# Stores of the transposed x1 in sixteen steps, down weights loaded behind the last form of x, and another order of operands in the out projection

## The chip, the cores and the metric

The kernel runs on one core of a Trainium2 chip. The metric is the device time of one execution in microseconds (us). The five engines of the core run their own instruction streams in order: TensorE (PE, matrix products), VectorE (DVE), ScalarE (ACT), GpSimd (POOL) and SyncE (SP, which here issues nearly all transfers). They meet through semaphores only.

## The reference

One layer of a decoder trunk on x of 1024 tokens by 1024 features, float32:

```python
x = x + gla_mixer(rms_norm(x, norm_mix), w_in, w_gk_up, b_gk, g_onorm, w_out)
x = x + sqrelu_mlp(rms_norm(x, norm_ffn), w_ff1, w_ff2)      # square(relu(h @ w_ff1)) @ w_ff2
return rms_norm(x, final_norm)
```

The mixer is a gated linear attention whose last product is `(o * silu(r)) @ w_out`. The MLP has 4096 hidden features.

## The kernel before, in words

**Products.** Every big product is 1024 x 1024 x 1024 in float32, computed as a Strassen-like scheme of seven steps (`step`, `chunks_of`): each step multiplies one *form* (a block, or a sum of blocks, of the left side) with one form of the right side. Each operand form is 512 x 512, kept as two buffers of the tag `big` (half 0 and half 1 of the contracted dimension), and each buffer holds a high part (written by ACT, L81) and the remainder (written by DVE, L82). A product of high and low parts takes three matmuls, so a step has 48 matmuls of 128 x 512: half 0 for four lanes, then half 1. There are eight `big` buffers, enough for the step that runs and the one that is made.

**Plan.** After the projections and the attention, `plan` lists nine products: the out projection (number 0), then for each of four chunks c of 1024 hidden features an *up* product (w_ff1, into the hidden tiles `hq`) and a *down* product (w_ff2, added to the result). They are called up0, down0, up1, down1 and so on here. During step `at` of product i, `operand` makes the forms of the next step: sums of blocks first, then the split into high and low. The letters of `turns` set the order in which the parts of an operand are written into the program: "W" splits the weights, "n" makes the weight sums for the step after, "x" and "X" sum and split the other side. Other engines than PE are ordered by a scheduler from that program; PE's order is written by hand.

**The other side of an up product.** up0 makes the seven forms of x1 and stores them to DRAM (`xw`). up1, up2 and up3 load them back (class `Stored`, L1030, two transfers of 1 MB for each step) and do no sums.

**Weights.** Weights of the next product are loaded in steps 5 and 6 (`load`, ahead of the operand in the program). Each is four blocks called 11, 12, 21, 22 of two halves with 512 KB; up weights use the tags wa (11, 21, and the temporary t) and wb (12, 22), down weights wb (11, 21) and wa (12, 22, and t). For down products the sums of weight blocks run on POOL: t = 12 - 11 for step 1, then t = 22 - t and 12 = 22 - 12 for step 2, later t = 21 - t, each in two halves. POOL also sums the up weights of up1 to up3.

**Transposing x1.** The residual x1 lies in DRAM by features (`xh`) and is needed by tokens (`xm`) at the end. For each of eight tiles of 128 features, `turn_load` loads it (L976), `turn_blocks` transposes 32 x 32 blocks on DVE (L980), and `turn_store` writes it to `xm` with four transfers of 32 x 32 x 32 elements, 128 KB each (L987). Before, each tile takes three neighbouring steps and a new tile starts at every step, from the last step of down0 to the second of down1. All these transfers, the loads of `xw` and the weights are issued by SP, in order.

Of the kernel before, what the change touches and what calls it, by code (L numbers as in the profile page):

```python
# [25 lines left out]
NC = FF // 1024  # L26
# [14 lines left out]
def order_after(tc, inst, other, wait=True):  # L41

    kind = mybir.DependencyClass.Sync if wait else mybir.DependencyClass.NoSync
    tc.add_manual_dep(inst.ins, other.ins.name, mybir.DependencyInfo(kind, mybir.DependencyReason.DATA),
                      reason="order of phases")
# [3 lines left out]
def hybrid_trunk(ctx: ExitStack, tc: tile.TileContext, x, xT, w_head, w_r, w_gk, w_up,  # L49
                 w_out, w_ff1, w_ff2, vecs, g_fin, out):  # L50
    nc = tc.nc
# [25 lines left out]
    last = {}  # L77
# [41 lines left out]
    def run(general):  # L119
# [8 lines left out]
        def half(hf):  # L128
            return slice(hf * 512, hf * 512 + 512)
# [102 lines left out]
        def step(n, lhs, rhs, sink, by_lane=False, between={}, fine=False):  # L232

            b = BANK[n]

            def product(lane, kp):
                kh, k = kp // 2, kp % 2
                if n in (0, 1, 5) and kp == 0:
                    bank[b, lane] = new("gl" if b == "U" or lane == 0 else "mm")
                ls = slice(lane * P, lane * P + P)  # L240
                mm3(bank[b, lane], lhs[kh][:, k, 0, ls], lhs[kh][:, k, 1, ls], rhs[kh][:, k, 0, :], rhs[kh][:, k, 1, :],
                    n in (0, 1, 5) and kp == 0, n in (3, 5, 6) and kp == 3, True)
                if kp == 3:
                    sink(n, lane, bank[b, lane])

            if by_lane:
                for lane in range(4):
                    for kp in range(4):
                        product(lane, kp)
                        for f in between.get((lane, kp), ()):  # L250
                            f()
            elif fine:
                for kp in range(4):
                    for lane in range(4):
                        product(lane, kp)
            else:
                for kh in range(2):
                    for lane in range(4):
                        product(lane, 2 * kh)
                        product(lane, 2 * kh + 1)  # L260

        def chunks_of(plan, ops, hooks, sinks, last_by_lane=False, turns={}):

            def operand(i, at):

                which, order = plan[i][2], plan[i][4]
                w, x_ = plan[i][which], plan[i][1 - which]
                made = {}  # L270
                for turn in turns.get((i, at), ("W", "n", "x", "X") if which == 0 else ("x", "X", "W", "n")):
                    if callable(turn):
                        turn()
                    elif turn == "x":
                        x_.sums(order[at])
                    elif turn == "X":
                        made[1 - which] = x_.split(order[at])
                    elif turn == "w":
                        w.sums(order[at])
                    elif turn == "W":  # L280
                        made[which] = w.split(order[at])
                    elif at + 1 < len(order):
                        w.sums(order[at + 1])
                return made[0], made[1]

            def load(i, names):
                if i < len(plan):
                    w = plan[i][plan[i][2]]
                    for name in names[w.s_form]:
                        w.load(name)  # L290

            if not ops:
                ops.append(operand(0, 0))
            for i, (_, _, _, sink, order) in enumerate(plan):
                for at, n in enumerate(order):
                    for f in hooks.get((i, at), ()):
                        f()
                    cur = ops.pop(0)
                    if at == 5:
                        load(i + 1, {True: ("11", "12"), False: ("11", "12", "22")})  # L300
                    if at == 6:
                        load(i + 1, {True: ("21", "22"), False: ("21",)})
                    nxt = (i, at + 1) if at + 1 < len(order) else (i + 1, 0)
                    if nxt[0] < len(plan):
                        ops.append(operand(*nxt))
                    for f in hooks.get((i, at, "then"), ()):
                        f()
                    here = {k[2:]: v for k, v in hooks.items() if len(k) == 4 and k[:2] == (i, at)}
                    final_step = last_by_lane and (i, at) == (len(plan) - 1, 6)
                    step(n, *cur, sinks.get((i, at), sink), bool(here) or final_step, here, (i, at) in fine_steps)  # L310
# [176 lines left out]
        class KeptX:  # L487

            s_form = False
# [297 lines left out]
        def g(f, *args):  # L787
            return lambda: f(*args)
# [44 lines left out]
        def r_last():  # L833

            for n in R_LAST:
                wr[n] = wR.split(n)
                if n == R_LAST[0] or not general:
# [4 lines left out]
        hooks = {(0, 1): (gk_first,), (0, 1, "then"): (gk_first_out,), (0, 3): (split_up,),  # L842
                 (0, 4): (g(token_rms, range(0, 4)),), (0, 5): (g(token_rms, range(4, 8)),),
                 (1, 0, 0, 3): (g(spread_rms, 0),),
                 (2, 4): (r_last,),
                 (1, 2): (x12_load,), (1, 4): (x12_split,), (1, 5): (g(gk_second, 0),),
                 (1, 5, 1, 3): (g(gk_second, 1),), (1, 5, 2, 3): (g(spread_rms, 1),)}
        if not general:
# [10 lines left out]
                          (2, 0, 3, 3): (g(prep_fast, 2, 1),), (2, 3, "then"): (g(prep_fast, 3, 1),),  # L859
                          (2, 4, 2, 1): (g(operands, 0, "mm"),)})  # L860
        chunks_of([(wqk, xq, 0, qk_into, PLAIN), (xk, wv, 1, v_into, PLAIN), (xr_, wR, 1, r_into, R_FIRST)], ops_a, hooks, {},
                  turns={(0, 1): ("X", split_gate, "W"), (0, 2): ("x", "X", "w", "W", lambda: last.update(sums=last["split"], s1=last["sum"], s1_low=last["low"]), "n"),
                         (0, 3): ("W", "x", "X", "n"), (2, 3): ("x", "X", "W", g(wR.sums, 3))})
# [58 lines left out]
        def from_down(c):  # L922
            def bring(a, b, kh, dst):
                f0 = 8 * c + 4 * a + 2 * kh
                nc.sync.dma_start(dst.rearrange("p (k n) -> p k n", k=2),
                                  w_ff2[f0:f0 + 2, :, half(b)].rearrange("k p n -> p k n"))
            return bring


# [33 lines left out]
        ops = [[wo.split(0), so.split(0)]]  # L963
# [8 lines left out]
        turn = {}  # L972
# [7 lines left out]
            dve.transpose(u, turn[kt])  # L980
            turn[kt] = u

        def turn_store(kt):
            u = turn.pop(kt)
            for q_ in range(4):
                dst = xm[:, kt * P + 32 * q_:kt * P + 32 * q_ + 32].rearrange("(b i) j -> i b j", i=32)
                store = nc.sync.dma_start(dst, u[32 * q_:32 * q_ + 32, :].rearrange("p (b j) -> p b j", j=32))  # L987
                order_after(tc, store, last["xw"], wait=False)
# [25 lines left out]
        xw = [[dram.tile([P, 2048], F32, name=f"xw{n}{kh}{int(general)}") for kh in range(2)] for n in range(7)]  # L1014
# [3 lines left out]
                nc.sync.dma_start(xw[n][kh], tiles[kh].rearrange("p k l t -> p (k l t)").bitcast(F32))  # L1018

        class Stored:  # L1020
            s_form = False

            def sums(self, n):
                pass
# [75 lines left out]
        plan = [(wo, so, 0, onto_x1T, PLAIN)]  # L1100
# [5 lines left out]
        def load_gfin():  # L1106
# [3 lines left out]
        hooks = {(0, 0, 3, 3): [g(outputs_T, TT - 1, ("mm", "mm"))],  # L1110
                 (0, 4, "then"): [g(times_g, "11", lane) for lane in range(4)], (2 * NC - 2, 0): [load_gfin]}

        for k in range(KT):
            for i, at, f in ((2 * NC - 6, 6 + k, turn_load), (2 * NC - 6, 7 + k, turn_blocks), (2 * NC - 6, 8 + k, turn_store),
                             (2 * NC - 2, 5 + k, x1_load), (2 * NC - 2, 7 + k, x1_onto)):
                hooks.setdefault((i + at // 7, at % 7, "then"), []).append(g(f, k))
        chunks_of(plan, ops, hooks, {}, last_by_lane=True)

    flag = sb.tile([P, 1], I32, name="flag")
    with tc.manual_schedule(engines={mybir.EngineType.PE}):  # L1120
        run(False)
# [66 lines left out]
```

## Time and profile before

| | before |
|---|---|
| runs | 1010.89 us median of 3 (1007.34 to 1010.99) |
| profiled execution, own time | 1010.57 us |
| its span, first to last instruction | 1008.7 us |
| granted TensorE clock, mean | 0.993 of full speed |
| HBM read and written | 146.62 MB and 46.14 MB |

The page's second part shows the span in 40 slices, a digit for each (the busy share in tenths); the three rows below are those of VectorE, GpSimd and the sixteen DMA engines. A slice is 25.2 us long, so the slices 23 to 25 are 555 to 630 us.

```profile
DVE  6995796778889999699564369974349966569965
POOL 0000010113430000214043033224141224242270
DMA  9899785576382257660336996344961125970004
```

The rows say which engines are loaded in which stage; what ends a wait is read from the groups and the timeline.

### The profile page before, as it was taken

To read this page: it belongs to the slowest core of one execution; us is meant where nothing else is said; L and a number is where in the kernel's file an instruction comes from. 1 tells how busy PE (TensorE), PEld (TensorE's weight loads), DVE (VectorE), ACT (ScalarE), POOL (GpSimd) and SP (SyncE) were. 2 spreads that over 40 slices of the span, in tenths; PEclk is the share of its full clock that TensorE was granted. 3 is DMA by queue.
4 is the path that set the end of the run, shared out by engine and by line. 5 is a ranking of instruction groups with operands and counts; after the bars stand their busy time and mean duration, and the time that the engine had idled before them with its cause. 6 is when DMAs were issued, how large, how long until landed. Compare 5 with 4: busy or idle time off the path is not lost.

```text
span 1008.7 us, 12239 instructions
## 1 busy us (share of the span) xinstructions
PE 986.9 (98%) x4508; PEld 821.5 (81%) x4508; DVE 752.5 (75%) x899; ACT 564.9 (56%) x858; POOL 229.3 (23%) x142
## 2 busy tenths in 40 slices
PE   9999999999999999999999989999999999999995
PEld 7788878889988888888888868888888888888884
DVE  6995796778889999699564369974349966569965
ACT  7685554787784466666434454332447333556455
POOL 0000010113430000214043033224141224242270
PEclk9999999999999999999999999999999999999998
DMA  9899785576382257660336996344961125970004
GB/s 264 314 322 369 288 294 193 204 247 209 118 286 78 84 209 292 250 233 19 89 136 232 273 323 136 90 120 174 340 250 49 53 73 210 363 285 39 1 1 171
DMA packets 135694, 193.65 MB, mean 192 GB/s; under 512 B 39240, under 2 KB 100808, under 8 KB 124104
## 3 DMA queue, kind: packets, MB, share of 16 engines
q1 hardware_dynamic: 135064, 192.37, 55.3%
q8 instruction: 37, 0.61, 0.2%
q10 hardware_dynamic: 560, 0.40, 0.1%
q14 instruction: 33, 0.27, 0.1%
HBM read 146.62 MB, written 46.14 MB: 191 GB/s over the span
## 4 chain that ended last, share of the span: by engine, by line
PE 78%; DVE 2%; DMA 2%; ACT 1%; issue 1%; SPq 0%; DVEq 0%; ACTq 0%
PE gl L70 53%; PE mm L70 24%; DMA big<-xw 1%; DMA wb<-in_w_out 1%; DVE big L82 1%; DVE vx L1074 0%; PE mm L636 0%; DMA wb<-in_w_ff 0%; ACT g L696 0%; PE mm L715 0%; ACT wb L81 0%; DVE vx L950 0%; PE gl L715 0%; DVE g L1094 0%; DVE g L705 0%
## 5 line engine op out<-in xcount | busy, mean ns | idle before, releaser
L70 PE MATMUL gl<-big,big 128*128 128x512 f32 x2712 | 632.5, 391 | 6.5 <-DMA big<-xw 4.5
L70 PEld LDWEIGHTS gl<-big,big 128*128 128x128 f32 x2712 | 510.2, 188 | 114.2 <-ACT big L81 5.7
L70 PE MATMUL mm<-big,big 128*128 128x512 f32 x1224 | 288.6, 389 | 0.2 <-ACT g L810 0.2
L70 PEld LDWEIGHTS mm<-big,big 128*128 128x128 f32 x1224 | 229.7, 188 | 48.3 <-ACT g L810 0.6
L82 DVE TENSOR_TENSOR big<-wa,big 128x1024 fp32r<-128x1024 f32 (+1 forms) x118 | 156.7, 1353 | 85.1 <-ACT big L81 81.3
L81 ACT ACTIVATE big<-wa 128x1024 fp32r<-128x1024 f32 (+1 forms) x118 | 118.3, 1039 | 116.1 <-PE gl L70 59.3
L184 POOL TENSOR_TENSOR wa<-wa,wa 128x1024 f32<-128x1024 f32 x28 | 78.8, 2821 | 145.7 <-DVE big L82 144.9
L184 POOL TENSOR_TENSOR wa<-wa,wb 128x1024 f32<-128x1024 f32 x14 | 42.9, 3069 | 296.9 <-DVE big L82 258.9
L82 DVE TENSOR_TENSOR big<-wb,big 128x1024 fp32r<-128x1024 f32 x50 | 63.3, 1284 | 34.8 <-ACT big L81 34.8
L82 DVE TENSOR_TENSOR big<-hq,big 128x1024 fp32r<-128x1024 f32 x48 | 61.4, 1291 | 34.9 <-ACT big L81 34.8
L81 ACT ACTIVATE big<-wb 128x1024 fp32r<-128x1024 f32 x50 | 51.0, 1052 | 58.2 <-PE gl L70 26.6
L81 ACT ACTIVATE big<-hq 128x1024 fp32r<-128x1024 f32 x48 | 48.6, 1052 | 45.4 <-PE gl L70 21.9
L81 ACT ACTIVATE big<-raw 128x1024 fp32r<-128x1024 f32 x42 | 43.3, 1056 | 52.2 <-DVE raw L184 22.1
L82 DVE TENSOR_TENSOR big<-raw,big 128x1024 fp32r<-128x1024 f32 x42 | 67.2, 1620 | 4.5 <-ACT big L81 4.3
L556 POOL COPY top<-g 128x4 f32<-128x4 f32 x8 | 10.1, 1264 | 181.7 <-DVE g L548 181.7
L184 POOL TENSOR_TENSOR wa<-wb,wa 128x1024 f32<-128x1024 f32 x14 | 41.1, 2945 | 40.0 <-DVE big L82 40.0
L1009 ACT ACTIVATE hq<-hq 128x1024 f32<-128x1024 f32 x24 | 25.4, 1057 | 36.5 <-DVE hq L1002 36.5
L678 POOL TENSOR_SCALAR g<-g,est 128x256 f32<-128x256 f32 x28 | 29.1, 1056 | 52.0 <-DVE g L675 33.0
L1000 ACT ACTIVATE hq<-gl 128x512 f32<-128x512 f32 x36 | 21.3, 593 | 20.2 <-PE gl L70 20.1
L70 PE MATMUL gl<-wb,wa 128*128 128x256 f32 x180 | 32.1, 310 | 0.0
L1047 DVE TENSOR_TENSOR vx<-gl,vx 128x512 f32<-128x512 f32 x44 | 29.1, 681 | 0.9 <-PE gl L70 0.8
L70 PEld LDWEIGHTS gl<-wb,wa 128*128 128x128 f32 x180 | 26.3, 190 | 2.0
(201 smaller groups left out, 884.5 us busy)
## 6 DMA issues: line engine op xcount, KB each, us to landing
big<-xw SPq DMA_DIRECT2D x42, 1024.0 KB, 7.1
big<-xv SPq DMA_DIRECT2D x20, 1024.0 KB, 5.8
xv<-big SPq DMA_DIRECT2D x14, 1024.0 KB, 8.6
xw<-big SPq DMA_DIRECT2D x14, 1024.0 KB, 4.8
wa<-in_w_ff SPq DMA_DIRECT2D x32, 256.0 KB, 4.1
wb<-in_w_ff SPq DMA_DIRECT2D x32, 256.0 KB, 3.4
wa<-in_w_ff SPq DMA_DIRECT2D x16, 512.0 KB, 5.2
wb<-in_w_ff SPq DMA_DIRECT2D x16, 512.0 KB, 5.1
```

Of the source, the lines that this page charges most:

```text
L70: pe.matmul(o, w, m, start=start, stop=stop, skip_group_check=partial)
L81: last["split"] = act.activation(hi, src, AF.Copy)
L82: last["low"] = dve.tensor_tensor(lo, src, f32(hi), op=ALU.subtract)
L184: op = self.eng.tensor_tensor(*(self.ap(b, kp, 2) for b in (o, x_, y_)), op=op)
L556: pool.tensor_copy(top[:, 8 * h + 4 * hf:8 * h + 4 * hf + 4].unsqueeze(2), a[:, :, P - 1:P])
L678: pool.tensor_scalar(S[:, vs], Z[:, vs], g, None, op0=ALU.mult)
L1000: act.activation(d, p_, AF.Copy)
L1009: act.activation(d2, d2, AF.Relu)
L1047: dve.tensor_tensor(yd, p_, yd, op=ALU.add)
```

## The change

Three things are edited. `chunks_of` writes the loads of the next weights behind the operand when the other side is `Stored`, and each load of down1 to down3 is ordered behind the last load of `xw` that was written. `turn_store` issues two of the four stores of a tile, so a tile's stores lie in two steps, and a new tile starts at every second step (to the third step of up2). In the out projection the operand's parts are written in another order.

```diff
@@ chunks_of
-                    if at == 5:
-                        load(i + 1, {True: ("11", "12"), False: ("11", "12", "22")})
-                    if at == 6:
-                        load(i + 1, {True: ("21", "22"), False: ("21",)})
+                    stored = getattr(plan[i][1], "stored", False)
+                    loads = {5: {True: ("11", "12"), False: ("11", "12", "22")}, 6: {True: ("21", "22"), False: ("21",)}}.get(at)
+                    if loads and not stored:
+                        load(i + 1, loads)
                     nxt = (i, at + 1) if at + 1 < len(order) else (i + 1, 0)
                     if nxt[0] < len(plan):
                         ops.append(operand(*nxt))
+                    if loads and stored:
+                        load(i + 1, loads)
@@ from_down(c), bring
-                nc.sync.dma_start(dst.rearrange("p (k n) -> p k n", k=2),
-                                  w_ff2[f0:f0 + 2, :, half(b)].rearrange("k p n -> p k n"))
+                load = nc.sync.dma_start(dst.rearrange("p (k n) -> p k n", k=2),
+                                         w_ff2[f0:f0 + 2, :, half(b)].rearrange("k p n -> p k n"))
+                if c:
+                    order_after(tc, load, last["xw"], wait=False)
@@ turn_store
-        def turn_store(kt):
-            u = turn.pop(kt)
-            for q_ in range(4):
+        def turn_store(kt, q0):
+            u = turn[kt]
+            for q_ in (q0, q0 + 1):
@@ class Stored
-            s_form = False
+            s_form, stored = False, True
@@ hooks
-            for i, at, f in ((2 * NC - 6, 6 + k, turn_load), (2 * NC - 6, 7 + k, turn_blocks), (2 * NC - 6, 8 + k, turn_store),
-                             (2 * NC - 2, 5 + k, x1_load), (2 * NC - 2, 7 + k, x1_onto)):
-                hooks.setdefault((i + at // 7, at % 7, "then"), []).append(g(f, k))
-        chunks_of(plan, ops, hooks, {}, last_by_lane=True)
+            for i, at, f in ((2 * NC - 6, 6 + 2 * k, (turn_load, k)), (2 * NC - 6, 7 + 2 * k, (turn_blocks, k)),
+                             (2 * NC - 6, 8 + 2 * k, (turn_store, k, 0)), (2 * NC - 6, 9 + 2 * k, (turn_store, k, 2)),
+                             (2 * NC - 2, 5 + k, (x1_load, k)), (2 * NC - 2, 7 + k, (x1_onto, k))):
+                hooks.setdefault((i + at // 7, at % 7, "then"), []).append(g(*f))
+        chunks_of(plan, ops, hooks, {}, last_by_lane=True,
+                  turns={(0, at): ("x", "X", "W", "n") if at == 1 else ("W", "x", "X", "n") for at in range(1, 7)})
```

**SP, end of up1.** The last form of x for up1 is `xw_2866` and `xw_2867`; the loads from `in_w_ff` are the weights of down1. Before:

```order
L1030 DMA big_4767<-xw_2862 128x2048
L1030 DMA big_4769<-xw_2863 128x2048
L987 DMA xm_2809<-g_4704 32x32x32 x4
L976 DMA g_4777<-xh_2806 128x1024
L925 DMA wb_4835<-in_w_ff 128x2x512
L925 DMA wb_4836<-in_w_ff 128x2x512
L925 DMA wa_4843<-in_w_ff 128x2x512
L925 DMA wa_4844<-in_w_ff 128x2x512
L1030 DMA big_4853<-xw_2866 128x2048
L1030 DMA big_4855<-xw_2867 128x2048
```

and now:

```order
L1034 DMA big_4753<-xw_2862 128x2048
L1034 DMA big_4755<-xw_2863 128x2048
L991 DMA xm_2809<-g_4621 32x32x32 x2
L1034 DMA big_4823<-xw_2866 128x2048
L1034 DMA big_4825<-xw_2867 128x2048
L927 DMA wb_4827<-in_w_ff 128x2x512
L927 DMA wb_4828<-in_w_ff 128x2x512
L927 DMA wa_4831<-in_w_ff 128x2x512
L927 DMA wa_4832<-in_w_ff 128x2x512
L927 DMA wa_4835<-in_w_ff 128x2x512
L927 DMA wa_4836<-in_w_ff 128x2x512
```

Two stores and no weights stand between the last two forms of x; the weights 11 (wb), 12 and 22 (wa) follow the last form. Block 12 of down1, which before had been issued four steps earlier, is among them. In up2 and up3 it is the same: before, the down weights stood between the forms of x, now all behind the last.

**DVE, from the last step of up1 into down1.** `raw` and `hq_...<-hq,hq` are the sums of hidden blocks for step 1 of down1, `big<-hq` and `big<-wb` the low parts for its step 0. Before:

```order
L184 TENSOR_TENSOR raw_5006<-hq_4738,hq_4667 128x1024
L184 TENSOR_TENSOR hq_4738<-hq_4508,hq_4738 128x1024
L184 TENSOR_TENSOR raw_5007<-hq_4738,hq_4667 128x1024
L184 TENSOR_TENSOR hq_4738<-hq_4508,hq_4738 128x1024
L980 STREAM_TRANSPOSE g_4861<-g_4777 128x1024
L82 TENSOR_TENSOR big_4925<-hq_4508,big_4925 128x2x512
L82 TENSOR_TENSOR big_4928<-hq_4508,big_4928 128x2x512
L82 TENSOR_TENSOR big_4931<-wb_4835,big_4931 128x2x512
```

and now:

```order
L184 TENSOR_TENSOR raw_4980<-hq_4724,hq_4657 128x1024
L82 TENSOR_TENSOR big_4899<-hq_4506,big_4899 128x2x512
L184 TENSOR_TENSOR hq_4724<-hq_4506,hq_4724 128x1024
L82 TENSOR_TENSOR big_4902<-hq_4506,big_4902 128x2x512
L184 TENSOR_TENSOR raw_4981<-hq_4724,hq_4657 128x1024
L184 TENSOR_TENSOR hq_4724<-hq_4506,hq_4724 128x1024
L82 TENSOR_TENSOR big_4905<-wb_4827,big_4905 128x2x512
```

The transpose has left this stretch; the low part of weight half 0, which step 0 of down1 needs, is still behind all four sums. In up2 to down2 and up3 to down3 the order on DVE at this place is unchanged.

**DVE, start of the out projection.** `g_2664` is the normed output of token tile 6, which PE transposes before the out projection starts; `wb_2814` is a block of `w_out`, `hq_278` the mixer's output. Before:

```order
L702 SCALAR_TENSOR_TENSOR st_2665<-st_2665 128x4
L82 TENSOR_TENSOR big_2868<-wb_2814,big_2868 128x2x512
L705 SCALAR_TENSOR_TENSOR g_2664<-gl_2666,st_2665,big_2170 128x256 x2
L705 SCALAR_TENSOR_TENSOR g_2664<-gl_2667,st_2665,big_2170 128x256 x2
L82 TENSOR_TENSOR big_2871<-wb_2815,big_2871 128x2x512
```

and now:

```order
L704 SCALAR_TENSOR_TENSOR st_2665<-st_2665 128x4
L82 TENSOR_TENSOR big_2868<-hq_278,big_2868 128x2x512
L707 SCALAR_TENSOR_TENSOR g_2664<-gl_2666,st_2665,big_2170 128x256 x2
L707 SCALAR_TENSOR_TENSOR g_2664<-gl_2667,st_2665,big_2170 128x256 x2
L701 TENSOR_SCALAR st_2754<-st_2754,tok_88 128x4
```

A split of the mixer's output stands where a split of a weight block stood.

## The prediction

> **What bounds the kernel now.** First the page's head and engine rows, then the waits of PE, longest first, then PE's timeline around the longest.
>
> ```profile
> span 1008.7 us, 12239 instructions
> PE 986.9 (98%) x4508; PEld 821.5 (81%) x4508; DVE 752.5 (75%) x899; ACT 564.9 (56%) x858; POOL 229.3 (23%) x142
> PE gl L70 <- DMA big<-xw: 4.5, 1, 4.5
> PE mm L715 <- DVE g L705: 1.5, 1, 1.5
> 583.06 4.24 PE L70 MATMUL mm<-big,big 128*128 128x512 f32 x18
> 587.14 11.04 PE L70 MATMUL gl<-big,big 128*128 128x512 f32 x48
> 602.73 12.47 PE L70 MATMUL gl<-big,big 128*128 128x512 f32 x42 [4.54 <-DMA big<-xw]
> 598.00:612.00 14.00, 9.46 (x30) 7.44 (x30) 13.71 (x8) 7.13 (x8) 9.00 (x4) 0.76 1.01 317
> 986.31 11.04 PE L70 MATMUL gl<-big,big 128*128 128x512 f32 x48
> ```
>
> PE is the bound; no other engine is near. So only what starves PE counts. Its pace: 18 matmuls from 583.06 to 587.14 are 0.2267 us each, so a step of 48 takes 10.88 (a row's duration is 0.16 longer, the tail of its last matmul). The last step of up1 should begin at 587.14 + 10.88 = 598.02; its first matmul comes at 602.73, **4.7 us** late. The 42 matmuls behind it take 12.47 - 0.16 = 12.3 instead of 9.5, **2.8 us** more: the window row (its last columns are granted clock, DMA share, GB/s) shows a clock of 0.76 there. One late transfer costs 7.5 us.
>
> Why it is late: the SP queue's timeline, then the landings of two pairs of `big<-xw`, an undisturbed one at 522 and this one.
>
> ```profile
> 580.37 8.26 SPq L987 DMA_DIRECT2D xm<-g  x4
> 590.37 0.91 SPq L925 DMA_DIRECT2D wb<-in_w_ff  x2
> 591.37 0.99 SPq L925 DMA_DIRECT2D wa<-in_w_ff  x2
> 592.45 1.10 SPq L1030 DMA_DIRECT2D big<-xw  x2
> L1030 SPq DMA_DIRECT2D big<-xw x2: 339/386/433, 522.1 to 522.4; - x2
> DMA to landing us min/median/max: 4.8/5.9/7.0
> L1030 SPq DMA_DIRECT2D big<-xw x2: 452/526/600, 592.4 to 593.0; - x2
> DMA to landing us min/median/max: 10.1/11.2/12.2
> ```
>
> Four stores hold SP for 8.3 us, two pairs of weights follow, and the last form is issued at 592.45, 5.3 us after its step began, behind queued data (10.1 us to landing instead of 4.8).
>
> **Part 1, the late form: -7.5 us at that place.** Two stores instead of four hold SP for about half of 8.3 us in a step of 10.88, and the weights come behind. The last form can then be issued at 587.3 and the second half lands at about 587.7 + 7.0 = 594.7, 3 us ahead of need. I take the whole 7.5.
>
> **Part 2, what is late next.** The same stretch on DVE and POOL (all times here stay on the clock of before):
>
> ```profile
> 598.83 2.65 DVE L184 TENSOR_TENSOR raw<-hq,hq 128x1024 f32<-128x1024 f32 x1
> 601.52 3.27 DVE L184 TENSOR_TENSOR hq<-hq,hq 128x1024 f32<-128x1024 f32 x1
> 604.70 3.38 DVE L184 TENSOR_TENSOR raw<-hq,hq 128x1024 f32<-128x1024 f32 x1
> 608.12 1.23 DVE L184 TENSOR_TENSOR hq<-hq,hq 128x1024 f32<-128x1024 f32 x1
> 612.66 2.35 DVE L82 TENSOR_TENSOR big<-wb,big 128x1024 fp32r<-128x1024 f32 x2
> 595.67 4.73 POOL L184 TENSOR_TENSOR wa<-wa,wb 128x1024 f32<-128x1024 f32 x2 [37.97 <-DMA wb<-in_w_ff]
> 600.34 6.66 POOL L184 TENSOR_TENSOR wa<-wa,wa 128x1024 f32<-128x1024 f32 x2
> ```
>
> A DVE sum takes 1.23 us alone and up to 3.38 while POOL sums: they alternate, one DVE instruction per POOL instruction, 3.3 us a pair. POOL's four weight sums (t in two halves, 12 in two halves) stretched DVE's chain so that the low part of weight half 0, without which step 0 of down1 can't run, was ready at 612.66 + 1.17 = 613.8. PE without the late form wants it at 598.02 + 10.88 = 608.9. **Behind the wait that goes stands another of 4.9 us**, hidden now only because PE is itself late.
>
> The change makes it longer. The weights are issued behind the last form, so their data come after 594.7. The pair at 592.45 landed 2.6 us apart (10.1 and 12.2 after issues 0.5 apart), 1 MB in 2.6 us, so 0.5 MB takes 1.3: 11 is there at 597.3, the halves of 12 at 598.6 and 599.9, of 22 at 601.2 and 602.5. All four POOL sums now fall behind 598.6, onto DVE's chain, which starts at 598.83. By the new order this chain is seven instructions down to the low part of `wb`: 7 x 1.15 = 8.05, and four POOL sums between them add 3.3 - 1.15 = 2.15 each, 8.6. End: 598.83 + 8.05 + 8.6 = 615.5, 6.6 us after 608.9. If the weights land a few us sooner or later the same four sums still fall into the chain. The clock: a wait of 4.7 was followed by 2.8 of slow matmuls; for one of 6.6 the bounds are 0 and 3.4 (half rate for as long as 0.24 x 14 / 0.5 = 6.7 us), and I take the row's 2.8. **+9.4 us.**
>
> The Trainium skill (TensorE: Matmul & The Clock Gate, "What's actually happening") says that the clock halves after an idle window of about 3.4 us and returns after a busy one. By that rule 6.6 us nearly always hold such a window, and the restart costs 1.7 to 3.4 (an estimate from that page's figure); the sum would be 1019.1 to 1020.8. The trace agrees with the halving (42 matmuls in 12.3 us).
>
> **Part 3, down2 and down3.** Before, the four sums ran well ahead of the last steps of up2 (from 757.8) and up3 (from 910.2), since the weights stood between the forms of x. These starts are 21 and 7 steps before 986.31, the last step's row.
>
> ```profile
> 733.23 3.31 POOL L184 TENSOR_TENSOR wa<-wa,wb 128x1024 f32<-128x1024 f32 x1 [15.72 <-DVE big L82]
> 885.55 5.67 POOL L184 TENSOR_TENSOR wa<-wa,wb 128x1024 f32<-128x1024 f32 x2 [15.72 <-DVE big L82]
> 891.18 4.75 POOL L184 TENSOR_TENSOR wa<-wa,wa 128x1024 f32<-128x1024 f32 x2
> 770.49 1.23 DVE L82 TENSOR_TENSOR big<-wa,big 128x1024 fp32r<-128x1024 f32 x1 [0.29 <-ACT big L81]
> 771.95 3.31 DVE L82 TENSOR_TENSOR big<-wa,big 128x1024 fp32r<-128x1024 f32 x1 [0.24 <-ACT big L81]
> 796.47 2.35 DVE L82 TENSOR_TENSOR big<-wa,big 128x1024 fp32r<-128x1024 f32 x2
> 948.76 1.22 DVE L82 TENSOR_TENSOR big<-wa,big 128x1024 fp32r<-128x1024 f32 x1
> ```
>
> Now all down weights follow the last form there too, and POOL's sums fall into the last step and step 0 of the down product. DVE has hardly an idle moment there (0.29, 0.24), so it carries 8.6 us of delay along, and what slack it has decides. The smallest is in step 3: in down2 its weight half is ready at 796.47 + 1.17 = 797.65, PE wants it 17 steps before 986.31, at 801.35: 3.7 us. In down3 948.76 + 1.22 = 949.98 against 953.67, three steps before: 3.7 again. **8.6 - 3.7 = +4.9 us each.** The bounds are 0 (idle moments, and additions that read PSUM, taking the delay up) and 5.9 (each POOL sum blocking DVE for its full 2.4).
>
> The rule that speaks against this change is in the Trainium skill (SBUF — State Buffer, "Who interferes with whom"): a VectorE instruction with two SBUF inputs and a GpSimd instruction that reads SBUF exclude each other, the second waits for the whole of the first. By it the sums cost DVE their full length wherever they meet; the rows agree (3.27, 3.38). If each were only slowed to half its pace, a DVE sum would take 2.3 beside POOL, four would add 4.6, and the total would be 1010.57 - 7.5 + 2.6 + 2.8 + 0.9 + 0.9 - 2.1 = 1008.2.
>
> **Part 4, the out projection: -2.1 us.** DVE at its start, the ACT row behind it, and PE:
>
> ```profile
> 297.47 0.15 DVE L702 SCALAR_TENSOR_TENSOR st<-st 128x4 f32<-128x4 f32 x1
> 299.27 1.23 DVE L82 TENSOR_TENSOR big<-wb,big 128x1024 fp32r<-128x1024 f32 x1 [1.65 <-ACT big L81]
> 300.42 1.65 DVE L705 SCALAR_TENSOR_TENSOR g<-gl,st,big 128x256 f32<-128x256 f32 x4
> 298.18 1.06 ACT L81 ACTIVATE big<-wb 128x1024 fp32r<-128x1024 f32 x1 [2.92 <-DMA wb<-in_w_out]
> 293.05 0.60 PE L715 MATMUL gl<-ident,g 128*128 128x128 f32 x4
> 298.93 0.59 PE L70 MATMUL gl<-g,hq 128*128 128x256 f32 x2
> 301.04 1.41 PE L715 MATMUL mm<-ident,g 128*128 128x128 f32 x4 [1.51 <-DVE g L705]
> 302.65 11.14 PE L70 MATMUL gl<-big,big 128*128 128x512 f32 x48
> 337.00 8.23 PE L70 MATMUL gl<-big,big 128*128 128x512 f32 x35 [0.33 <-DVE big L82]
> ```
>
> PE waits for L705, which stands behind a split that waits for a weight from DRAM. Now the split of `hq` stands there, and ACT, idle 2.92 us, can make its high part by 296.3. So L705 starts at 297.6 + 1.2 = 298.8, its four parts (0.41 each) end at 300.5, the last of the first four transposes and the four behind it (0.60 - 0.16 = 0.44 for four) follow, and the product begins at about 301.1 instead of 302.65: 1.55. The 0.5 around 337.00 (low part of x late by one sum of weights, now behind it) goes too. Bounds 0 and 3.1 (all of both waits: two matmuls from 298.93 on and eight transposes end at 300.1, 2.6 earlier).
>
> The moved transposes and stores I price at nothing: there are as many as before, two stores and a load in a step of 10.88 leave SP free for half of it, and the last store, now in step 2 of up2, still stands before the first load of `xm`. What hides them is that free half; without it the forms of x come late again (third rival). The added order puts no wait on SP, it only moves the weights back in its queue.
>
> **Sum.** The profiled execution's own time is 1010.57 (0.3 under the median shown): 1010.57 - 7.5 + 9.4 + 4.9 + 4.9 - 2.1 = **1020.2**.
>
> **The rivals.**
> - *The wait simply goes (faster).* DVE is not what PE waits for: the weights arrive early enough, or the sums do not block DVE. For it: the change removes PE's longest wait. Against: 613.8 stands in the trace. It decides if POOL is done before 598. 1010.57 - 7.5 - 2.1 = 1001.0. Chance 0.12.
> - *The wait moves, down2 and down3 swallow theirs (no change).* 1010.57 - 7.5 + 9.4 - 2.1 = 1010.4, if idle moments absorb over 5 of 8.6 us. Chance 0.20, with what lies between.
> - *The change does not do what it says.* Two stores with full DMA queues still hold SP, the last form stays late, and the wait for DVE hides behind it: 1010.57 + 9.8 - 2.1 = 1018.3. Chance 0.05.
>
> My forecast, the sum, has 0.63. The range reaches from 1006 (part of the faster case and all between left out) to 1024 (5.9 for each of down2 and down3, 0.6 more for the clock, nothing gained at 337, and 0.7 less at 301). A measurement of this kernel can tell about 0.5%, 5 us: faster (under 1005.8) 0.12, the same 0.20, slower (over 1015.9) 0.68, the forecast and the third rival.
>
> **What would show it.** Right: no wait for `big<-xw`; the first wait of PE is at step 0 of down1 for DVE's `big<-wb`, 6 to 7 us with a lower clock behind it; POOL's `wa<-wa,wb` begin after the last step of up2 and up3 has; DVE rows of 3.3 us in step 0 of down2 and down3, and PE waits of 1 to 3 us in their first four steps; L705 before 299. Wrong: POOL's sums ahead of the last up step, or DVE sums of 1.2 us beside them.

## The result, and the profile after

The changed kernel takes 1021.34 us in the median of 4 runs (1020.56 to 1023.26), the kernel before, run beside it, 1010.94 us (1007.34 to 1012.77). The ratio is 1.011 with a 95% interval of 1.0079 to 1.0141: slower, by more than the half per cent that can be told apart. The prediction was 1020.2 us.

The page's head and engine row and the longest waits of PE (in total, times, longest, in us) are now:

```profile
span 1019.6 us, 12233 instructions
PE 991.6 (97%) x4508; PEld 825.0 (81%) x4508; DVE 765.7 (75%) x899; ACT 563.6 (55%) x858; POOL 231.8 (23%) x142
PE gl L70 <- ACT hq L1008: 9.2, 2, 4.6
PE gl L70 <- DVE big L82: 6.9, 2, 6.5
```

The wait for `big<-xw` has gone from the list; a wait for DVE and two for ACT stand there now. Where they lie is read from the start of each product's first matmul in the two traces (lengths in us; products that are not in the table differ by nothing):

| | before | after | difference | predicted |
|---|---|---|---|---|
| start of the out projection's product | 302.65 | 300.04 | -2.61 | -1.55 |
| out projection | 77.78 | 77.21 | -0.57 | -0.5 |
| up1 | 83.65 | 76.16 | -7.49 | -7.5 |
| down1 | 76.16 | 84.95 | +8.79 | +9.4 |
| down2 | 76.16 | 83.05 | +6.89 | +4.9 |
| down3 | 75.93 | 83.39 | +7.46 | +4.9 |
| last matmul to the end of the span | 11.8 | 10.1 | -1.6 | 0 |
| span | 1008.7 | 1019.6 | +10.9 | +9.6 |

The first six differences add up to 12.47, and the last matmul starts 12.48 us later: nothing else moved. The last row is the final store of the output, which took 5.9 us after its issue instead of 7.5; over all the runs below this row lies between 10.2 and 11.6 without a pattern that follows the edits, and what sets it was not looked into.

**up1 into down1.** PE, the window's row (its last columns are granted clock, DMA share, GB/s), and the issue and landing of the last form:

```profile
583.97 22.15 PE L70 MATMUL gl<-big,big 128*128 128x512 f32 x97
612.65 12.70 PE L70 MATMUL gl<-big,big 128*128 128x512 f32 x46 [6.53 <-DVE big L82]
606.00:622.00 16.00, 9.47 (x33) 7.55 (x33) 15.43 (x12) 6.00 (x8) 5.38 (x2) 0.79 0.12 22
584.17 0.99 SPq L1034 DMA_DIRECT2D big<-xw  x2
DMA to landing us min/median/max: 4.8/5.9/6.9
```

97 matmuls run without a pause from step 5 of up1 to the first matmul of down1: the form, issued at 584.17, is there well before 594.85, where the last step of up1 begins. The second matmul of down1 is the first to read the low part of the weights, and it waits until 612.65. DVE and POOL in that stretch:

```profile
595.66 1.22 DVE L184 TENSOR_TENSOR raw<-hq,hq 128x1024 f32<-128x1024 f32 x1
596.79 3.43 DVE L82 TENSOR_TENSOR big<-hq,big 128x1024 fp32r<-128x1024 f32 x1
600.15 3.43 DVE L184 TENSOR_TENSOR hq<-hq,hq 128x1024 f32<-128x1024 f32 x1
603.50 3.42 DVE L82 TENSOR_TENSOR big<-hq,big 128x1024 fp32r<-128x1024 f32 x1
606.84 3.36 DVE L184 TENSOR_TENSOR raw<-hq,hq 128x1024 f32<-128x1024 f32 x1
610.23 1.23 DVE L184 TENSOR_TENSOR hq<-hq,hq 128x1024 f32<-128x1024 f32 x1
611.37 2.36 DVE L82 TENSOR_TENSOR big<-wb,big 128x1024 fp32r<-128x1024 f32 x2
596.42 6.07 POOL L184 TENSOR_TENSOR wa<-wa,wb 128x1024 f32<-128x1024 f32 x2 [41.89 <-DMA wa<-in_w_ff]
602.46 6.66 POOL L184 TENSOR_TENSOR wa<-wa,wa 128x1024 f32<-128x1024 f32 x2
```

Four DVE instructions take 3.4 us instead of 1.2, one for each POOL sum between 596.42 and 609.12; the low part of `wb` is the last of seven.

**down2** (down3 reads the same): PE, ACT, DVE and POOL.

```profile
772.95 3.36 PE L70 MATMUL gl<-big,big 128*128 128x512 f32 x7 [4.59 <-ACT hq L1008]
761.61 1.06 ACT L81 ACTIVATE big<-raw 128x1024 fp32r<-128x1024 f32 x1 [1.38 <-PE gl L70]
771.36 1.06 ACT L81 ACTIVATE big<-raw 128x1024 fp32r<-128x1024 f32 x1 [8.69 <-DVE raw L184]
772.32 0.58 ACT L1008 ACTIVATE hq<-gl 128x512 f32<-128x512 f32 x1
757.90 3.45 DVE L82 TENSOR_TENSOR big<-wb,big 128x1024 fp32r<-128x1024 f32 x1
761.28 3.42 DVE L184 TENSOR_TENSOR hq<-hq,hq 128x1024 f32<-128x1024 f32 x1
764.62 3.41 DVE L82 TENSOR_TENSOR big<-wb,big 128x1024 fp32r<-128x1024 f32 x1
767.96 3.36 DVE L184 TENSOR_TENSOR raw<-hq,hq 128x1024 f32<-128x1024 f32 x1
757.42 6.20 POOL L184 TENSOR_TENSOR wa<-wa,wb 128x1024 f32<-128x1024 f32 x2 [36.37 <-DMA wa<-in_w_ff]
763.58 6.66 POOL L184 TENSOR_TENSOR wa<-wa,wa 128x1024 f32<-128x1024 f32 x2
```

Step 0 of down2 begins at 766.85, and its seventh matmul, the first of lane 1, needs a PSUM bank that still holds a tile of up2. The evacuation that frees it (L1008, 772.32) stands on ACT behind the split of `raw`, which waits 8.69 us for a DVE sum that POOL has delayed (four DVE rows of 3.4 us beside four POOL sums, as in down1). PE has the operands; it lacks the bank.

### The profile page after: what moved, and what is told of

It reads as the page before. It is cut to its first block, busy times and chain, and to the rows that moved or that the text cites. A ratio compares the mean times of both kernels' runs of the same rounds, so it can differ in the third digit from the quotient of the medians.

```text
span 1019.6 us, 12233 instructions
## 1 busy us (share of the span) xinstructions
PE 991.6 (97%) x4508; PEld 825.0 (81%) x4508; DVE 765.7 (75%) x899; ACT 563.6 (55%) x858; POOL 231.8 (23%) x142
## 4 chain that ended last, share of the span: by engine, by line
PE 77%; DVE 6%; ACT 2%; issue 1%; DVEq 0%; ACTq 0%
PE gl L70 51%; PE mm L70 25%; DVE big L82 2%; DVE raw L184 1%; DVE hq L184 1%; DVE vx L1078 0%; PE mm L638 0%; ACT g L698 0%; PE mm L717 0%; ACT big L81 0%; ACT wb L81 0%; DVE big L785 0%; PE gl L717 0%; DVE g L1098 0%; DVE g L707 0%
## 5 line engine op out<-in xcount | busy, mean ns | idle before, releaser
L184 POOL TENSOR_TENSOR wa<-wa,wa 128x1024 f32<-128x1024 f32 x28 | 82.6, 2959 | 103.8 <-DVE big L82 103.1
L82 DVE TENSOR_TENSOR big<-hq,big 128x1024 fp32r<-128x1024 f32 x48 | 65.9, 1381 | 33.1 <-ACT big L81 33.0
L82 DVE TENSOR_TENSOR big<-wb,big 128x1024 fp32r<-128x1024 f32 x50 | 71.2, 1442 | 26.0 <-ACT big L81 25.9
L82 DVE TENSOR_TENSOR big<-raw,big 128x1024 fp32r<-128x1024 f32 x42 | 64.7, 1559 | 4.6 <-ACT big L81 4.6
L558 POOL COPY top<-g 128x4 f32<-128x4 f32 x8 | 7.2, 896 | 182.0 <-DVE g L550 182.0
L1004 ACT ACTIVATE hq<-gl 128x512 f32<-128x512 f32 x36 | 21.4, 595 | 36.4 <-PE gl L70 36.3
## 6 DMA issues: line engine op xcount, KB each, us to landing
wa<-in_w_ff SPq DMA_DIRECT2D x16, 512.0 KB, 10.2
```

The source lines that it names most:

```text
L82: last["low"] = dve.tensor_tensor(lo, src, f32(hi), op=ALU.subtract)
L184: op = self.eng.tensor_tensor(*(self.ap(b, kp, 2) for b in (o, x_, y_)), op=op)
L558: pool.tensor_copy(top[:, 8 * h + 4 * hf:8 * h + 4 * hf + 4].unsqueeze(2), a[:, :, P - 1:P])
L1004: act.activation(d, p_, AF.Copy)
```

## The experiments

Four runs take the change apart, four more test what holds PE in the down products, and two split the weights' edit. Ratios are to the kernel before on the same chip; where it is a sum of products, the lengths are those of the traces as in the table above.

### The three parts, each alone

Stores alone (the piece of `turn_store` and the loop over `KT`):

```diff
-        def turn_store(kt):
+        def turn_store(kt, q0):
...
+            for i, at, f in ((2 * NC - 6, 6 + 2 * k, (turn_load, k)), (2 * NC - 6, 7 + 2 * k, (turn_blocks, k)),
+                             (2 * NC - 6, 8 + 2 * k, (turn_store, k, 0)), (2 * NC - 6, 9 + 2 * k, (turn_store, k, 2)),
```

> Only the stores are spread; the weights of down1 still stand ahead of the last form of x. Theory (POOL's weight sums stretch the DVE chain where they meet it): SP is held for two stores instead of four, so weights and form are issued some 6 us earlier than before. The 7.5 us at the last form of up1 go, POOL is done with its sums before most of the DVE chain, and no wait of over 2 us comes at step 0 of down1: about 1003 us, 7.5 under before, and down2 and down3 show no wait. Rival (the DVE chain is late whatever the weights do): a wait of 4.9 us for DVE at step 0 of down1, 1008 us or more.

Weights alone:

```diff
+                    if loads and stored:
+                        load(i + 1, loads)
...
+                if c:
+                    order_after(tc, load, last["xw"], wait=False)
```

> Only the weights of down1 to down3 are moved behind the last form; four stores a step and the order of the out projection as before. Theory: down2 and down3 lose what they lose in the changed kernel, 7.0 and 7.6 us with the slow clock behind the waits, in step 0, where PE waits for ACT. At up1 the form is issued about 2 us earlier than before and without weights ahead of it, so its wait falls to 0 to 1 us, and the sums of weights fall into the DVE chain of down1: 9 to 11 us there. Sum 1010.9 - 7 + 10 + 14.6 = 1028 us (1025 to 1032). Rival (the loss belongs to the moved transposes and stores, not to the weights): about 1004 to 1011.

Out projection alone:

```diff
+        chunks_of(plan, ops, hooks, {}, last_by_lane=True,
+                  turns={(0, at): ("x", "X", "W", "n") if at == 1 else ("W", "x", "X", "n") for at in range(1, 7)})
```

> Only the order of operands in the out projection is changed. Theory: the product begins 2.6 us earlier and the loss at 337 us goes, all else as before: 1010.9 - 2.6 = 1008 us (1007.5 to 1009). Rival (the gain is taken back later in the out projection, where the sums now stand elsewhere): 1010.9, no change.

Stores and out projection, without the weights (the two diffs together):

> The stores are spread and the out projection is reordered, the weights stay where they were. Theory: the gains of the two add, 1010.9 - 7.5 - 2.6 = 1000.8 us. Rival (the wait at up1 only moves to DVE at down1): 1005 to 1006 us.

| | median us | ratio, 95% interval | up1 | down1 | down2 | down3 |
|---|---|---|---|---|---|---|
| stores | 1000.24 | 0.9894 (0.9877 to 0.991) | 76.16 | 76.16 | 76.16 | 75.93 |
| weights | 1022.50 | 1.0102 (1.0083 to 1.0121) | 76.16 | 85.38 | 83.26 | 83.51 |
| out projection | 1007.08 | 0.9966 (0.9952 to 0.9981) | 82.20 | 76.16 | 76.16 | 75.93 |
| stores and out projection | 998.52 | 0.9871 (0.9852 to 0.9889) | 76.16 | 76.16 | 76.16 | 75.93 |
| all three | 1021.34 | 1.011 (1.0079 to 1.0141) | 76.16 | 84.95 | 83.05 | 83.39 |

Either the stores or the weights alone take the wait for the form away. The stores do it without a price, the weights with all of it: over the kernel with stores and out projection, the weights' edit adds 8.79 + 6.89 + 7.46 = 23.1 us, and the medians are 22.8 apart.

The weights alone came out 5.5 us under the 1028 expected and missed its range: their products cost 16.4 us in the trace (-7.5 + 9.2 + 7.1 + 7.6) where 17.6 had been put down, the out projection began 1.1 earlier and the last store was 1.6 shorter, and the median lies 1.7 under the profiled execution (1024.19). The stores alone, and both together, came 2.8 and 2.3 us under their 1003 and 1000.8: beside the 7.5 us of up1 (and the 0.57 of the out projection in the second), the product of the out projection begins 1.4 and 2.5 earlier than in the profile of before, and the last store is 1.6 and 1.5 shorter. The out projection alone came 0.4 under its range; 1.45 us of its gain is the late form of up1, which cost less than before (last section).

Why the stores alone cost nothing behind the form is seen in the run with the out projection, at the same place as above:

```profile
585.04 5.75 POOL L184 TENSOR_TENSOR wa<-wa,wb 128x1024 f32<-128x1024 f32 x2 [30.40 <-DVE hq L1002]
590.75 5.75 POOL L184 TENSOR_TENSOR wa<-wa,wa 128x1024 f32<-128x1024 f32 x2
595.77 1.82 DVE L184 TENSOR_TENSOR raw<-hq,hq 128x1024 f32<-128x1024 f32 x1
598.77 1.22 DVE L184 TENSOR_TENSOR raw<-hq,hq 128x1024 f32<-128x1024 f32 x1
603.43 2.35 DVE L82 TENSOR_TENSOR big<-wb,big 128x1024 fp32r<-128x1024 f32 x2
```

Here SP issues the weights at 575.97 to 582.5, ahead of the form, POOL is done at 596.5, and DVE's chain has 1.2 us an instruction behind its first row. The low part is ready at 604.6; PE begins down1 at 605.84 and reads it with the second matmul.

### Two of POOL's sums less

```diff
-                    for o, x_, op, y_ in self.form[n][1]:
+                    for o, x_, op, y_ in self.form[n][1][:1] if self.eng is pool and not self.s_form else self.form[n][1]:
```

> The changed kernel without the second sum of weight blocks (12 = 22 - 12) on POOL in the down products: block 12 itself is used in its place, two POOL sums of each down product are left out. The order on DVE and ACT is that of the changed kernel. Theory (each POOL sum costs the DVE instruction beside it 2.2 us): the chain is 4.4 us shorter in each of the three places. Wait at down1 6.7 to 2.3 us, at down2 and down3 4.75 to about 0.4 us, and without a wait over 3 us the slow clock goes too: down1 2.3, down2 and down3 0.4 us over a product without waits, 1001 us in all. Rival (the weights' data are late, the sums only stand beside): no change, 1021 us. Rival (each is only slowed to half its pace): 2.3 us less in each place and the slow clock stays at down1: about 1011 us.

1004.3 us, ratio 0.9952 (0.9933 to 0.9971): 3 us over the 1001 expected. The profiled execution took 1002.75, the shortest of the seven; its down products are as expected to 0.2 us, and its last store is 1.0 longer than in the changed kernel's profile. Why the other executions are longer still is not shown. DVE, POOL and PE at down1:

```profile
596.75 3.44 DVE L82 TENSOR_TENSOR big<-hq,big 128x1024 fp32r<-128x1024 f32 x1
600.12 3.42 DVE L184 TENSOR_TENSOR hq<-hq,hq 128x1024 f32<-128x1024 f32 x1
603.47 1.21 DVE L82 TENSOR_TENSOR big<-hq,big 128x1024 fp32r<-128x1024 f32 x1
606.99 2.35 DVE L82 TENSOR_TENSOR big<-wb,big 128x1024 fp32r<-128x1024 f32 x2
596.63 5.83 POOL L184 TENSOR_TENSOR wa<-wa,wb 128x1024 f32<-128x1024 f32 x2 [42.14 <-DMA wa<-in_w_ff]
608.26 12.32 PE L70 MATMUL gl<-big,big 128*128 128x512 f32 x53 [2.18 <-DVE big L82]
```

Two stretched DVE rows instead of four, and PE's second matmul comes at 608.26 instead of 612.65: 4.35 us less of a wait (the start of down1 differs by 0.03), 2.2 for each POOL sum. The down products are 78.64, 76.69 and 76.45 long, 2.5, 0.5 and 0.5 over those without a wait, where 2.3, 0.4 and 0.4 were expected. The weights landed as late as before, so it is the sums and not the data that PE waits for, and a sum costs DVE nearly its own length, not half.

### The order on DVE and on ACT

DVE's sums of hidden blocks behind the low parts, for step 1 of a down product:

```diff
-                        if n == 4 and self.late is True and "low" in last:
+                        if n == 1 and self.behind or n == 4 and self.late is True and "low" in last:
                             order_after(tc, op, last["low"], wait=False)
...
+        for c in range(1, NC):
+            plan[2 * c + 2][0].behind = True
```

> The changed kernel, with DVE's sums of hidden blocks for step 1 of down1 to down3 ordered behind the low parts for step 0. Theory: the low part of weight half 0 of down1 then stands third in DVE's chain instead of seventh, and the wait of 6.7 us with the slow clock behind it goes (8.8 us). In down2 and down3 the second sum into raw is still the fourth or fifth DVE instruction beside POOL, ACT stalls on it as before, and their 6.9 and 7.5 us stay: 1021.3 - 8.8 = 1012.5 us. Rival (PE waits there for data that land late, not for its place in DVE's queue): down1 as before, 1021 us.

ACT's split of `raw` behind the last evacuation:

```diff
+                    if n == 1 and self.evac:
+                        order_after(tc, last["split"], last["out"], wait=False)
...
-                        act.activation(d, p_, AF.Relu)
+                        last["out"] = act.activation(d, p_, AF.Relu)
...
+        for c in range(1, NC):
+            plan[2 * c + 2][0].evac = True
```

> The changed kernel, with ACT's split of raw for step 1 of down1 to down3 ordered behind the last evacuation (L1008) of the up product. Theory: in down2 and down3 PE waits for a PSUM bank that ACT can't free while it stands at that split; with the evacuations ahead, the waits in step 0 go, and DVE's delay is taken up before it reaches PE: 1021.3 - 6.9 - 7.5 = 1007 us, with down1 as before (8.8). Rival (the prediction's: DVE's delay of 8.6 us meets a slack of 3.7 in step 3): waits of 3.6 to 4.9 us come in step 3 of down2 and down3 in their place, 1014 to 1017 us.

Both together:

> The changed kernel with both orders: DVE's sums of hidden blocks behind the low parts, and ACT's split of raw behind the last evacuation. Theory: all three waits go although the weights still come behind the last form of x and POOL's sums still fall beside DVE's chain: 1021.3 - 8.8 - 6.9 - 7.5 = 998 us, as with the stores and the out projection alone. Rival (the DVE work is simply too much there, and the delay comes out in a later step): waits of 2 to 5 us in steps 1 to 3 of the down products, 1004 to 1013 us.

| | median us | ratio, 95% interval | down1 | down2 | down3 |
|---|---|---|---|---|---|
| low parts first (DVE) | 1012.37 | 1.0022 (1.0002 to 1.0041) | 79.15 | 82.09 | 79.77 |
| evacuations first (ACT) | 1013.25 | 1.0029 (1.001 to 1.0048) | 85.43 | 78.24 | 78.03 |
| both | 1010.16 | 0.9999 (0.9984 to 1.0013) | 79.15 | 80.42 | 78.55 |

PE in down2 with the evacuations first, then PE in down1 with the low parts first:

```profile
764.68 15.58 PE L70 MATMUL gl<-big,big 128*128 128x512 f32 x68
...
801.29 0.50 PE L70 MATMUL gl<-big,big 128*128 128x512 f32 x1 [0.64 <-ACT big L81]
802.67 1.42 PE L70 MATMUL gl<-big,big 128*128 128x512 f32 x5 [0.87 <-DVE big L82]
618.35 1.43 PE L70 MATMUL gl<-big,big 128*128 128x512 f32 x5 [0.66 <-DVE big L82]
...
642.13 1.42 PE L70 MATMUL gl<-big,big 128*128 128x512 f32 x5 [1.26 <-DVE big L82]
```

With the evacuations first, PE runs through step 0 of down2 (which begins at 767.86) without a pause: the wait was ACT's order. But at step 3, from 801.29, the same delay of DVE arrives after all, 2.1 us in down2 and 2.1 in down3. Theory and rival were each half right: 1007 and 1014 to 1017 were expected, 1013.25 came. The waits of step 3 are shorter than the rival's 3.6 to 4.9 because DVE has made up a part by then: its low part for step 3 is ready 34.7 us after the start of down2, in the kernel before 28.9 (797.64 - 768.71), so it is 5.8 late and not 8.6; less the slack of 3.7 that is the 2.1 that came. With the low parts first, the wait of 6.7 us in step 0 of down1 goes, and 3.0 us come back in steps 1 to 3. That its time (1012.37) equals the one expected is chance: down1 lost 3.0 instead of nothing, and down2 and down3 lost 5.9 and 3.8 instead of 6.9 and 7.5. Both orders together leave 3.0, 4.3 and 2.6 us, in steps 1 to 3, as their rival said. So the late sums are the cause and the two orders only choose where it shows: put right, they recover 11 of 23 us by the medians.

### The two halves of the weights' edit

Written behind the operand, without the added order:

```diff
-                if c:
-                    order_after(tc, load, last["xw"], wait=False)
```

> The changed kernel without the added order in from_down: the weights are still written behind the operand. SP's order at up1 is that of the changed kernel, and in up2 and up3 blocks 12 and 22 still stand behind the last form of x (11 ahead of it). Theory: POOL's first sum needs 12, so nothing is won: down1 +8.8, down2 and down3 +6.9 and +7.5 as in the changed kernel, 1021 us. Rival (the added order does the harm): the loss goes, 998 to 1001 us.

The added order, with the loads written ahead of the operand as before:

```diff
+                    if at == 5:
+                        load(i + 1, {True: ("11", "12"), False: ("11", "12", "22")})
+                    if at == 6:
+                        load(i + 1, {True: ("21", "22"), False: ("21",)})
...
-                    if loads and stored:
-                        load(i + 1, loads)
```

> Stores spread and out projection reordered, and the added order in from_down, but the loads are written ahead of the operand as before. Then the weights stay ahead of the last form in up2 and up3 and only block 12 of down1 moves, to just ahead of the last form of up1. Theory: down2 and down3 show no wait; at up1 the form, which landed just in time without this (10.8 us after its issue at 584.27, wanted at 594.96), stands behind 1 MB more, which takes about 2.6 us, so a wait of 0 to 2.7 us comes there, or it is taken up by the second half's later need: 998.5 to 1001.5 us. Rival (the added order does the harm): 1015 us or more.

The first takes 1011.59 us (ratio 1.0017, 0.9999 to 1.0035), the second 1004.65 (0.9949, 0.9931 to 0.9968). Both expectations missed. With the place alone, down1 and down2 lose 6.9 and 6.2 us, but down3 nothing: there POOL's sums run from 888.05 to 898.43, ahead of up3's last step, which begins at 912.65. With the order alone no down product loses anything, but up3 becomes 5.0 us longer (up1 1.1). DVE, POOL and PE at the end of step 5 of up3:

```profile
896.02 2.32 DVE L114 SCALAR_TENSOR_TENSOR rstd<-st,rstd 128x1 f32<-128x1 f32 x1
898.37 2.32 DVE L1061 TENSOR_TENSOR ss<-rstd 128x1 f32<-128x1 f32 x1
900.73 3.35 DVE L1062 SCALAR_TENSOR_TENSOR vx<-vx,ss,g 128x1024 f32<-128x1024 f32 x1
904.00 2.47 DVE L1004 TENSOR_TENSOR hq<-gl,hq 128x512 f32<-128x512 f32 x4
895.93 2.40 POOL L184 TENSOR_TENSOR wa<-wa,wb 128x1024 f32<-128x1024 f32 x1
898.28 4.72 POOL L184 TENSOR_TENSOR wa<-wa,wa 128x1024 f32<-128x1024 f32 x2
904.79 3.53 PE L70 MATMUL gl<-big,big 128*128 128x512 f32 x10 [3.17 <-issue]
```

The added order puts the six weight transfers of down3 next to each other, later than before, and POOL's sums of them land on other work of DVE: two instructions of one column, 0.16 us each where no POOL sum stands beside them, take 2.32. Behind them stand the additions that empty PSUM (L1004, four of 0.6 us from 904.00 on), and PE goes on 0.8 us after the first of these starts. The profile names no releaser for this wait; that it is the bank again is read from the times (for the wait of 0.9 us at the same place of up1 it names DVE's L1004). So neither half of the edit is free, and both pay through the same pair of engines.

## Why the prediction was right, and where it was not

- **The late form** (-7.5): right, -7.49, and the form was issued and landed ahead of need as worked out.
- **The DVE chain behind it** (+9.4): right in place, path and size: +8.79. The wait is 6.7 (6.6 was worked out from seven instructions and four POOL sums); the slow clock cost 2.1 instead of 2.8, for a reason given below. Two sums less shortened it by 4.35, so the price of a sum, 2.15, holds.
- **down2 and down3** (+4.9 each): the cause was right, the path not. The step that failed is "The smallest is in step 3" and "8.6 - 3.7 = +4.9 us each", together with "PE waits of 1 to 3 us in their first four steps" and no slow clock. DVE's delay was as worked out, but before step 3 it passes through ACT. The rows of before show it:

```profile
763.18 1.22 DVE L184 TENSOR_TENSOR raw<-hq,hq 128x1024 f32<-128x1024 f32 x1
763.47 2.02 ACT L81 ACTIVATE big<-raw 128x1024 fp32r<-128x1024 f32 x2 [1.37 <-PE gl L70]
765.40 0.58 ACT L1004 ACTIVATE hq<-gl 128x512 f32<-128x512 f32 x1
```

  ACT frees the bank at 765.98, right behind the split of the second sum, which DVE ends at 764.40. PE wants the bank at the seventh matmul of step 0, 768.71 + 6 x 0.2267 = 770.07, a slack of 4.1. After the change the sum ends at 771.32, which is 773.18 on the clock of before (up2's last step begins 1.86 us earlier): 8.8 late, less 4.1 is 4.7, and the trace has 4.75 and 4.73. Behind each of these waits the clock is halved as well, 2.1 and 2.7 us more, which the forecast had left out. The slack of step 3 is real, as the run with the evacuations first shows, but it stood second, and what got past it was 2.1, not 4.9, since DVE's delay had shrunk to 5.8 by then in that run: "so it carries 8.6 us of delay along" did not hold there either.
- **The out projection** (-2.1): -3.2 in this profile, and the surplus is not the edit's. DVE and PE at its start in the changed kernel:

```profile
297.82 1.65 DVE L707 SCALAR_TENSOR_TENSOR g<-gl,st,big 128x256 f32<-128x256 f32 x4
298.50 1.35 PE L717 MATMUL mm<-ident,g 128*128 128x128 f32 x4
```

  From the two matmuls ahead of these transposes (298.93 before, 298.07 now) to the start of the product it took 3.71 us and now takes 1.97. It takes 1.97 in all nine profiles with the reordered parts, and 2.91, 3.71 and 4.28 in the three without. So the edit gained 1.74 here, where 1.55 was worked out, and L707 starts before 299 as forecast; PE still waits a little, since its transposes follow the parts of L707 one by one (1.35 us for four instead of 0.60). The other 0.86 was there ahead of this place: these two matmuls come anywhere from 297.30 to 298.98 over the profiles, with the edit and without, and why was not looked into. The rest (0.57) is the loss at 337 that went.
- **The sum** came within 1.1 us in part by luck, because errors cancel: 4.6 too little for down2 and down3 against 0.6 too much for down1, 1.1 too little gain in the out projection and 1.6 us of the last store.
- **The rivals.** "The wait simply goes" is what the stores do, 1000.24 us alone and 998.52 with the out projection, where 1001.0 was given. Its condition, POOL done before 598 where the last step of up1 begins, was stricter than needed: with the stores and the out projection POOL ends at 596.5, 1.5 us behind that point (594.96 there), and only the first row of DVE's chain is longer (1.82). Without its weights the change would have been this case. That two stores still hold SP too long was wrong.

The version that beats both kernels is the one with stores and out projection: 998.52 us, 1.3% under the kernel before.

## What to carry to other kernels

A transfer that is late can be cured by moving what stands ahead of it or by making that smaller; before moving it, ask when its own consumers start and which engine they then run beside. A delay on one engine is to be followed through every queue that waits for it, and the smallest slack counted along each: here it reached PE not by its operands but by an evacuation behind a stalled split on ACT. And an edit in three parts is to be priced in three parts, since two of these gained 12.7 us and the third, on top of them, lost 22.8.

## What the runs showed of the hardware

The slow clock has a length of its own. In the record of the granted clock, half-speed stretches within the products are 3.41 or 6.83 us long, and those of one run start a multiple of 3.413 us apart (610.01, 770.44 and 930.87 in the changed kernel: 47 times 3.413 each). What a wait costs beside itself is half of the stretch that is left when PE comes back:

| run, place | half speed from, to | PE back at | half of the rest | loss beyond the wait |
|---|---|---|---|---|
| before, up1 | 601.62, 608.45 | 602.73 | 2.86 | 2.8 |
| after, down1 | 610.01, 616.84 | 612.65 | 2.10 | 2.10 |
| after, down2 | 770.44, 777.27 | 772.95 | 2.16 | 2.14 |
| after, down3 | 930.87, 937.69 | 932.14 | 2.78 | 2.73 |
| out projection alone, up1 | 600.01, 603.43 | 599.90 | 1.71 | 1.7 |

In the last row PE came back just before the stretch began, and one length was enough; this, and a wait shorter by 0.35, is why the same late form cost up1 7.5 us in the kernel before and 6.0 there. The Trainium skill (TensorE: Matmul & The Clock Gate, "What's actually happening") calls the activity window behind the clock free-running, and these starts agree.

What was new is that a wait need not fill such a window of 3.41 us. In down2 of the changed kernel PE idled 2.2 of the 3.41 us before the stretch at 770.44, and with the low parts first 2.1 of those before the stretch at 924.51 in down3: both times the clock was halved. With the evacuations first, 1.9 us in two pieces (step 3 of down2) did not halve it. Nor did the wait of 2.34 us in the run with two sums less: counted in steps of 3.413 from the stretch at its end (993.49), a window ends at 607.78, so that 1.86 us of the wait lie in one window and 0.48 in the next. The "wait over 3 us" of that run's expectation is therefore not the condition. Of the windows at full speed within the nine products of these profiles, each one with 2.1 us idle or more was followed by half speed, and none with 1.9 or less.
